# The first two tiles of a decoder step run side by side, chunk by chunk of x, behind four products of ones

## The chip, the core and the metric

One core of a Trainium2 chip runs the whole program in one launch. The metric is the device time of that launch in microseconds. The engines are named as the profile names them: PE is TensorE, PEld its weight load, DVE is VectorE, ACT is ScalarE, POOL is GpSimd, SP is SyncE (here it issues nearly all DMAs). `L491` is line 491 of the kernel before.

## What is computed

The reference is one step of a two-layer decoder trunk over 512 prompt tokens and 32 sample tokens, all in float32. The change touches only the start of the first SwiGLU block:

```python
def rmsnorm(x, g):
    y = x * lax.rsqrt(jnp.mean(x * x, axis=-1, keepdims=True) + EPS)
    return y * g

def swiglu(x, w1, w3, w2):
    return (jax.nn.silu(x @ w1) * (x @ w3)) @ w2

# layer i: half SwiGLU -> token mixer -> half SwiGLU -> gated embedding
h = h + 0.5 * swiglu(rmsnorm(h, ffn1_norm[i]), ffn1_w1[i], ffn1_w3[i], ffn1_w2[i])
```

## The kernel before

The residual stream `h` lies transposed: eight chunks of 128 features (partitions) by 544 tokens. Every product is made in three passes for float32 accuracy. Each operand is split in a high part (a cast to the multiply type, on ACT) and a low part (what is left over, on DVE), and PE multiplies high by high, high by low, low by high. `prep` (L297, L298) applies the norm's gain to a chunk of x and splits it. `_split` (L198, L199) splits one piece of weights: 128 by 1024 numbers, 512 KB. The rsqrt factor of the norm is applied later, to the result.

A **tile** is one output of 128 rows by 544 tokens in PSUM: eight chunks, three passes each, and every pass is a pair of matmuls over 256 and 288 columns (`mm`, L241, L245, L247), so 24 pairs. The first SwiGLU block starts with eight such plain tiles (`ffn`, with `plain` = 2, from the w1 and w3 columns in turn); after them comes a seven-product (Strassen) scheme at L491. Its products come in the order 1, 5, 6, 2, 7, 3, 4. Product 6 adds into the PSUM tile of product 1, so it has to wait until ACT has copied product 1 out (L499). Plain tiles have three PSUM buffers; ACT copies each finished tile out (L426), which frees its buffer.

The sums of squares for the norm (squares on ACT L1357, adds on DVE L1359) go through four matmuls with a matrix of ones (L362) and then through a chain on ACT (L340) and DVE (L343 to L347). That chain gives the factor `rstd`, and the gates (L451, L454, L457) and the operands of the seven-product scheme (L307, L311 to L314, L285, L286) stand behind or between it on the same two engines. In the kernel before, `tile_rstd` runs these four matmuls inside the first tile for which the loop of `ffn` asks; the scheduler puts them into the third tile.

What sets the order: each engine runs its own list in order. In the blocks under `manual_schedule` the list of the named engines is the order of the code; elsewhere the scheduler of the framework places instructions by its own estimate. DMAs of SP go out in SP's order, and at most eight of them can be open, since the ninth waits on the semaphore of the first. SP's list also holds register loads from a page table `pt` (L1030, a TENSOR_LOAD and two small instructions each), which wait until `pt` has landed and stand between the DMAs. Weights are loaded piece by piece in the order in which the tiles use them. I call them piece 0, 1, 2 and so on; tile 1 uses piece 0.

Of the kernel before, what the change touches and what calls it, by code (L numbers as in the profile page):

```python
# [22 lines left out]
F32 = mybir.dt.float32  # L23
F32R = mybir.dt.float32r
I32 = mybir.dt.int32
AF = mybir.ActivationFunctionType
ALU = mybir.AluOpType
AX = mybir.AxisListType

P = 128  # L30
D = 1024
NC_ = D // P
# [57 lines left out]
def whole(p):  # L90

    return p[:].rearrange("p a b -> p (a b)")[:, 512 - CUT:512 - CUT + T]


class Builder:
# [310 lines left out]
    def ffn(self, h, box, gcol, rstd, on_chunk, plain=1):  # L406

        nc, eng = self.nc, mybir.EngineType
        self.ahead = (2, 3, 6)
        first, xs, xf = [], self.pairs(box), box["f"]  # L410

        def more(n):
            if len(xf) < min(n, NKP):
                xf.append(self.forms(h, gcol, len(xf), xs))
        hid, todo = {}, ([], [])
        lead = plain == 1 and len(xf) < 3
        for f in range(2 * plain):
            g = self.big()
            for w in range(2):
                if lead:  # L420
                    more(len(xf) + 1)
                if rstd is None:
                    p, rstd = self.tile_rstd(xs, box["acc"])
                else:
                    p = self.tile_mm(xs)
                nc.scalar.copy(g[:, w], whole(p))  # L426
                for t in todo:
                    if t:
                        t.pop(0)()
                if not lead:  # L430
                    more((2 * f + w + 1) // plain)
            first.append((f // 2, f % 2, g))
            if f % 2 and f < 2 * plain - 1 or lead and f == 0:
                for j, a, g in first:
                    todo[a].extend(self.gate(hid, rstd, j, a, g))
                first = []
        assert self.chain is None
        for j, a, g in first:
            todo[a].extend(([None] * 3 if j == 0 else []) + self.gate(hid, rstd, j, a, g))
        with self.tc.manual_schedule(engines={eng.PE, eng.Activation, eng.DVE, eng.Pool}):  # L440
            self.ffn_steps(h, xf, rstd, hid, todo, plain, on_chunk)
        self.ahead = (2, 2, 4)
        self.pins = 2
        return rstd
# [853 lines left out]
    def build(self):  # L1298
        nc, i, o = self.nc, self.i, self.o
# [26 lines left out]
        nc.vector.memset(self.eps, EPS)  # L1326
        warm = self.sm(1)
        nc.scalar.copy(warm, self.eps)
        self._load()
        self.g = self.const.tile([P, NG], F32, name="gains")  # L1330
        nc.scalar.dma_start(out=self.g, in_=i["gains"])
        hp = [self.big() for _ in range(NC_ // 2)]
        h = [hp[c // 2][:, c % 2, :] for c in range(NC_)]
        for c in range(NC_):
            nc.sync.dma_start(out=h[c], in_=i["x"][c])
            if c == 2:
                self._load()
        self.ones = self.const.tile([P, 32], F32, name="ones")
        nc.gpsimd.memset(self.ones, 1.0)
        self.onesr = self.const.tile([P, P], F32R, name="onesr")  # L1340
# [8 lines left out]
        box = {"x": {}, "f": [], "acc": self.st()}  # L1349
        with self.tc.manual_schedule(engines={mybir.EngineType.Activation, mybir.EngineType.DVE}):  # L1350
            for c in range(NC_):
                box["x"][c] = self.prep(h[c], G_FFN1 + c)
                if c in (0, NC_ - 1):
                    self._split()
            for c in range(NC_):
                sq = box["acc"] if c == 0 else self.tmp()
                nc.scalar.activation(sq, h[c], AF.Square)  # L1357
                if c:
                    nc.vector.tensor_tensor(box["acc"], box["acc"], sq, ALU.add)  # L1359

        def constants():
            yield
            nc.sync.dma_start(out=self.c, in_=i["consts"])
            nc.sync.dma_start(out=self.pt, in_=i["pt"])
            passed = self.big()[:].rearrange("p a b -> p (a b)")
            nc.sync.dma_start(out=passed[:, :NPASS], in_=i["passed"])
            yield
            nc.gpsimd.tensor_copy(self.identr, self.ident)
            nc.gpsimd.tensor_copy(self.neg, passed[:, C_NEG:C_NEG + 384])
        self.bg.append(constants())  # L1370

        on, nxt = self.next_norm(h, G_MIX)
        self.ffn(h, box, G_FFN1, None, on, PLAIN[0])
        box = nxt
        on, nxt = self.next_norm(h, G_FFN2, early={1: 0, 3: 1, 5: 2})
        self.gmlp(h, box, on)
        box = nxt
        on, nxt = self.next_norm(h, G_PLE)
        self.ffn(h, box, G_FFN2, None, on)
        box = nxt  # L1380
# [3 lines left out]
        box = nxt  # L1384
        box, rstd = self.kv(h, box, G_FFN1 + 8)
        on, nxt = self.next_norm(h, G_MIX + 8)
        self.ffn(h, box, G_FFN1 + 8, rstd, on)
        box = nxt
        on, nxt = self.next_norm(h, G_FFN2 + 8, early={5: 0, 6: 1})
        self.attention(self.pairs(box), box["acc"], h, on)  # L1390
        box = nxt
        on, nxt = self.next_norm(h, G_PLE + 8)
        self.ffn(h, box, G_FFN2 + 8, None, on)
        box = nxt
# [120 lines left out]
```

## Time and profile before

| What | us |
|---|---|
| median of 3 runs (lowest, highest) | 2065.02 (2064.10, 2067.02) |
| the profiled execution | 2064.99 |
| its span, first to last instruction | 2063.2 |
| PE busy in the span | 2043.9 (99%) |
| DVE busy | 1507.6 (73%) |
| ACT busy | 949.2 (46%) |
| start of PE's first product | 6.94 |

The span leaves 1.8 us of the profiled execution outside. A row of a timeline says when a run of equal instructions started, how long it lasted from the first start to the last end, the engine, the line, and in brackets how long the engine had been idle and who ended that. Rows of matmuls overlap: a matmul's length includes the way through the array, and the distance between starts is the pace.

### The profile page before, as it was taken

The numbers are of one execution on the slowest core, as the hardware profiler recorded it, in microseconds if no ns is written. First come the engines' busy times: TensorE is split into PE (matmuls) and PEld (weight loads), VectorE is DVE, ScalarE is ACT, GpSimd is POOL, SyncE is SP. The second block draws the span as 40 slices with busy tenths as digits, with TensorE's granted clock in tenths as the row PEclk, the third lists the DMA queues.
The fourth block names the chain that finished last, engine by engine and source line by source line (L and its number), as shares of the span: only waits on it lengthen the run. The fifth ranks groups of instructions, "written<-read, shape, count | busy, mean of one in ns | idle before, by whom it ended". The sixth has DMA issues, their size and how long they took to land.

```text
span 2063.2 us, 38844 instructions
## 1 busy us (share of the span) xinstructions
PE 2043.9 (99%) x16432; PEld 2012.0 (98%) x16432; DVE 1507.6 (73%) x1869; ACT 949.2 (46%) x1405; POOL 186.9 (9%) x238
## 2 busy tenths in 40 slices
PE   8999999999999999999999999999999999999999
PEld 8999999999999999999999999999987999999999
DVE  7877777556687777776688777776476888777774
ACT  7534344423554344454456343434364754344451
POOL 0000000410100000043060000001142200000020
PEclk9999999999999999999999999999999999999999
DMA  5233234312223232432374322324669322322431
GB/s 185 84 110 108 73 108 141 97 44 83 83 92 113 73 106 80 153 99 82 109 260 156 112 93 102 108 71 130 201 208 305 103 101 82 104 103 82 128 99 44
DMA packets 93807, 237.95 MB, mean 115 GB/s; under 512 B 9522, under 2 KB 27474, under 8 KB 93634
## 3 DMA queue, kind: packets, MB, share of 16 engines
q1 hardware_dynamic: 93490, 235.44, 34.4%
q8 instruction: 129, 2.11, 0.4%
q14 instruction: 44, 0.36, 0.1%
q10 hardware_dynamic: 144, 0.04, 0.0%
HBM read 218.95 MB, written 16.49 MB: 114 GB/s over the span
## 4 chain that ended last, share of the span: by engine, by line
PE 93%; DVE 3%; ACT 2%; issue 1%; DMA 1%; SPq 0%; POOL 0%; DVEq 0%; ACTq 0%
PE ps L491 33%; PE ps L241 16%; PE ps L247 16%; PE ps L245 16%; PE pb L491 5%; DVE big L199 1%; PE ps L1265 1%; PE ps L1269 1%; PE ps L1268 1%; ACT big L198 1%; PE ps L1222 0%; DVE big L184 0%; PE ps L829 0%; PE ps L830 0%; PE ps L831 0%
## 5 line engine op out<-in xcount | busy, mean ns | idle before, releaser
L491 PE MATMUL ps<-big,big 128*128 128x272 f32 x5616 | 727.7, 288 | 1.8 <-DVE big L508 1.3
L491 PEld LDWEIGHTS ps<-big,big 128*128 128x128 f32 x5616 | 714.2, 188 | 2.4 <-issue 1.6
L199 DVE TENSOR_TENSOR big<-big,big 128x1024 fp32r<-128x1024 f32 (+2 forms) x538 | 592.2, 1103 | 106.6 <-ACT big L198 106.0
L198 ACT CAST big<-big 128x1024 fp32r<-128x1024 f32 (+2 forms) x538 | 488.0, 932 | 267.8 <-DVE big L184 262.8
L241 PE MATMUL ps<-big,big 128*128 128x256 f32 (+1 forms) x2684 | 559.0, 289 | 7.2 <-ACT big L198 7.2
L247 PE MATMUL ps<-big,big 128*128 128x256 f32 x2684 | 554.5, 288 | 1.3 <-DVE big L199 1.3
L245 PE MATMUL ps<-big,big 128*128 128x256 f32 x2684 | 554.0, 287 | 0.0
L241 PEld LDWEIGHTS ps<-big,big 128*128 128x128 f32 x2684 | 430.5, 189 | 10.7 <-ACT big L198 7.4
L245 PEld LDWEIGHTS ps<-big,big 128*128 128x128 f32 x2684 | 432.9, 189 | 0.0
L247 PEld LDWEIGHTS ps<-big,big 128*128 128x128 f32 x2684 | 429.8, 188 | 3.1 <-DVE big L199 2.7
L326 POOL TENSOR_TENSOR st<-st,tmp 128x544 f32<-128x544 f32 (+1 forms) x63 | 87.4, 1387 | 1589.1 <-ACT tmp L324 1589.0
L530 DVE SCALAR_TENSOR_TENSOR big<-ps,big 128x544 f32<-128x544 f32 x160 | 115.6, 723 | 106.5 <-PE ps L247 106.4
L184 DVE TENSOR_TENSOR big<-big,big 128x1024 f32<-128x1024 f32 x156 | 190.1, 1219 | 0.0
L499 ACT COPY tmp<-ps 128x544 f32<-128x544 f32 x117 | 71.7, 613 | 141.3 <-PE ps L491 141.3
L454 ACT ACTIVATE big<-big 128x544 f32<-128x544 f32 x88 | 58.0, 660 | 163.3 <-DVE big L451 162.1
L491 PE MATMUL pb<-big,big 128*128 128x272 f32 x936 | 124.0, 288 | 0.0
L451 DVE TENSOR_TENSOR big<-big,st 128x1088 f32<-128x1088 f32 x88 | 113.7, 1293 | 10.6 <-ACT big L513 8.9
L491 PEld LDWEIGHTS pb<-big,big 128*128 128x128 f32 x936 | 120.2, 188 | 0.0
L297 ACT ACTIVATE big<-big,gains 128x544 fp32r<-128x544 f32 (+1 forms) x80 | 55.8, 704 | 118.4 <-DVE big L530 64.9
L286 DVE TENSOR_TENSOR big<-big,big 128x544 fp32r<-128x544 f32 (+1 forms) x112 | 80.9, 728 | 36.2 <-ACT big L285 36.1
L298 DVE SCALAR_TENSOR_TENSOR big<-big,gains,big 128x544 fp32r<-128x544 f32 (+1 forms) x80 | 66.0, 832 | 26.1 <-ACT big L297 26.1
L285 ACT CAST big<-big 128x544 fp32r<-128x544 f32 (+1 forms) x112 | 71.3, 644 | 16.0 <-DVE big L457 8.9
(208 smaller groups left out, 1435.6 us busy)
## 6 DMA issues: line engine op xcount, KB each, us to landing
big<-in_w SPq DMA_DIRECT2D x156, 512.0 KB
big<-in_w2a SPq DMA_DIRECT2D x64, 512.0 KB
big<-in_w2b SPq DMA_DIRECT2D x32, 384.0 KB
big<-in_w13p SPq DMA_DIRECT2D x16, 512.0 KB
big<-in_win SPq DMA_DIRECT2D x16, 512.0 KB
big<-in_wg SPq DMA_DIRECT2D x16, 512.0 KB
big<-in_ck SPq DMA_DIRECT2D x16, 512.0 KB
big<-in_cv SPq DMA_DIRECT2D x16, 512.0 KB
```

Of the source, the lines that this page charges most:

```text
L184: self.nc.vector.tensor_tensor(t, a, b, ALU.add if op == "+" else ALU.subtract)
L198: self.nc.scalar.copy(hi, src)
L199: self.nc.vector.tensor_tensor(lo, src, hi.bitcast(F32), ALU.subtract)
L241: i = nc.tensor.matmul(out[:, a:b], wh, xh[:, a:b], start=s, stop=False)
L245: nc.tensor.matmul(out[:, a:b], wh, xl[:, a:b], start=False, stop=False)
L247: nc.tensor.matmul(out[:, a:b], wl, xh[:, a:b], start=False, stop=e)
L286: self.nc.vector.tensor_tensor(pair[:, 1, cols], src, pair[:, 0, cols].bitcast(F32), ALU.subtract)
L326: nc.gpsimd.tensor_tensor(acc[:, cols], acc[:, cols], sq, ALU.add)
L451: tt(g, g, rstd.unsqueeze(1).broadcast_to([P, 2, T]), ALU.mult)
L491: nc.tensor.matmul(dst[w], a[:, c], b, start=k in "152" and kp == 0 and n == 0, stop=kp == NKP - 1 and n == 2, skip_group_check=True)
L499: nc.scalar.copy(t["r" + k], t["C" if k == "5" else "A"])
L530: nc.vector.scalar_tensor_tensor(h[c], whole(out), 0.5, h[c], ALU.mult, ALU.add)
```

## The change

Three things change at the start of the program. First, PE gets four float32 products of a 128 by 256 tile of ones, whose result nobody reads, at the head of its list. Second, the first two weight pieces are no longer loaded whole around x. Each is loaded in two halves of 256 KB, and the halves are put between the chunks of x (behind chunks 0, 2, 3 and 5); ACT and DVE split a half as they come to it. Third, PE runs tiles 1 and 2 in turn: three chunks of tile 1, three of tile 2, then chunk 3 of both, chunk 4 of both, and so on. The loop of `ffn` takes these two tiles as done, so that its first call of `tile_rstd` comes with tile 3.

```diff
@@ ffn
             for w in range(2):
                 if lead:
                     more(len(xf) + 1)
-                if rstd is None:
+                if box.get("p"):
+                    self.prepare()
+                    p = box["p"].pop(0)
+                elif rstd is None:
                     p, rstd = self.tile_rstd(xs, box["acc"])
@@ build
-        self._load()
+        busy = self.flat(256)
+        nc.vector.memset(busy, 1.0)
+        t = self.pb()
+        for _ in range(4):
+            nc.tensor.matmul(t[:, :256], busy[:, :P], busy, start=True, stop=True)
+        w0 = [(self.flat(1024), self.flat(1024, F32R), self.flat(1024, F32R)) for _ in range(2)]
+        half = lambda k: slice(512 * k, 512 * k + 512)
         for c in range(NC_):
             nc.sync.dma_start(out=h[c], in_=i["x"][c])
-            if c == 2:
-                self._load()
+            for w, k in {0: [(0, 0)], 2: [(1, 0)], 3: [(0, 1)], 5: [(1, 1)]}.get(c, ()):
+                nc.sync.dma_start(out=w0[w][0][:, half(k)], in_=self.aps[w][:, half(k)])
+        self.a_load = self.p_split = self.p_sum = self.p_next = 2
@@ under manual_schedule of ACT and DVE
                 box["x"][c] = self.prep(h[c], G_FFN1 + c)
-                if c in (0, NC_ - 1):
-                    self._split()
+                for w, k in {0: [(0, 0)], 2: [(1, 0)], 3: [(0, 1)], 5: [(1, 1)]}.get(c, ()):
+                    raw, hi, lo = (t[:, half(k)] for t in w0[w])
+                    nc.scalar.copy(hi, raw)
+                    nc.vector.tensor_tensor(lo, raw, hi.bitcast(F32), ALU.subtract)
+            self._split()
@@ before the call of ffn
+        xs, b = self.pairs(box), [self.blocks(t[1:]) for t in w0]
+        box["p"] = [self.ps(), self.ps()]
+        with self.tc.manual_schedule(engines={mybir.EngineType.PE}):
+            for w, cs in ((0, range(3)), (1, range(3))) + tuple((w, [c]) for c in range(3, NC_) for w in range(2)):
+                self.mm(box["p"][w], [b[w][c] for c in cs], [xs[c] for c in cs], cs[0] == 0, cs[-1] == NC_ - 1)
```

How the lists of the engines move, at three places. The first is ACT behind the squares of x. Before, it casts piece 2 (`big_168`), copies tiles 1 and 2 out (`ps_182`, `ps_256`), makes the high part of the sum of squares (L357) and casts piece 3 (`big_174`):

```order
L1357 ACTIVATE tmp_163<-big_89 128x544
L198 CAST big_170<-big_168 128x1024 [waits DMAHW5_49]
L426 COPY big_167<-ps_182 128x544 [waits PE_49]
L426 COPY big_167<-ps_256 128x544 [waits PE_49]
L357 CAST tmp_225<-st_109 128x544 [waits DVE_49]
L198 CAST big_246<-big_174 128x1024 [waits DMAHW6_49]
```

After the change piece 2 is cast ahead of the squares; behind them stand the casts of piece 3 (`big_288`) and piece 4 (`big_294`), and only then the copies of tiles 1 and 2 (`ps_186`, `ps_187`):

```order
L1371 ACTIVATE tmp_182<-big_94 128x544
L198 CAST big_290<-big_288 128x1024 [waits DMAHW0_49]
L198 CAST big_296<-big_294 128x1024 [waits DMAHW1_49]
L429 COPY big_287<-ps_186 128x544 [waits PE_49]
L429 COPY big_287<-ps_187 128x544 [waits PE_49]
L307 ACTIVATE big_310<-big_91,gains 128x544 x2
```

So the copy of tile 1, which frees the PSUM buffer that tile 4 takes, now stands behind a cast that waits for the DMA of piece 4.

The second place is SP, from the constants and the page table `pt` on. Before, two register loads from `pt` stand ahead of the DMA of piece 2 (`big_168`):

```order
L1363 DMA consts<-in_consts 128x224 [waits DMAHW3_49]
L1364 DMA pt<-in_pt 1x16 [waits DMAHW4_49]
L1030 TENSOR_LOAD pt [waits DMAHW4_49]
L1030 ISA x2
L1030 TENSOR_LOAD pt
L1030 ISA x2
L165 DMA big_168<-in_w13p 128x1024 [waits DMAHW5_49]
```

After the change piece 2 (`big_157`) goes out ahead of the first register load:

```order
L1377 DMA consts<-in_consts 128x224 [waits DMAHW5_49]
L1378 DMA pt<-in_pt 1x16 [waits DMAHW6_49]
L165 DMA big_157<-in_w13p 128x1024 [waits DMAHW7_49]
L1033 TENSOR_LOAD pt [waits DMAHW6_49]
L1033 ISA x2
```

Piece 2 moved ahead of the loads. Behind it, five register loads now stand ahead of piece 3 and nine more ahead of piece 4, and six more ahead of piece 5; before, two stood ahead of piece 2, nine between pieces 2 and 3, and none between pieces 3, 4, 5 and 6.

The third place is PE where the four matmuls with ones for the norm (L362) stand. Before, they are inside tile 3 (`ps_331`), at its chunks 4 to 6:

```order
L247 MATMUL ps_331<-big_128,big_171 128x288
L362 MATMUL pb_229<-tmp_225,onesr 128x272 [waits Activation_49,Pool_49]
L362 MATMUL pb_230<-tmp_225,onesr 128x272
L241 MATMUL ps_331<-big_131,big_170 128x256
L241 MATMUL ps_331<-big_131,big_170 128x288
```

After, they are inside tile 5 (`ps_474`), at its first chunk and its second:

```order
L241 MATMUL ps_474<-big_125,big_296 128x256 [waits Activation_49]
L241 MATMUL ps_474<-big_125,big_296 128x288
L245 MATMUL ps_474<-big_125,big_296 128x256
L362 MATMUL pb_372<-tmp_368,onesr 128x272 [waits Activation_49,Pool_49]
L362 MATMUL pb_373<-tmp_368,onesr 128x272
```

They moved back by almost two tiles, and the chain for `rstd` with them. In the rows behind tile 8 the lists of PE, ACT and DVE are those of before, apart from a few neighbours that change places on DVE.

## Rows read from the trace of the kernel before

**Rows 1.** The page, its first line.

```profile
span 2063.2 us, 38844 instructions
```

**Rows 2.** PE's waits, whole span: who waited for whom, us, times, longest.

```profile
PE ps L241 <- ACT big L198: 7.2, 2, 6.9
PE pb L1241 <- DVE tmp L1237: 1.3, 1, 1.3
```

**Rows 3.** PE's timeline, tiles 1 and 2 and the start of tile 3.

```profile
6.94 0.82 PE L241 MATMUL ps<-big,big 128*128 128x256 f32 x2 [6.94 <-ACT big L198]
...
12.45 0.66 PE L247 MATMUL ps<-big,big 128*128 128x256 f32 x2
12.90 0.59 PE L241 MATMUL ps<-big,big 128*128 128x256 f32 x2
13.33 0.41 PE L245 MATMUL ps<-big,big 128*128 128x256 f32 x2
...
22.05 0.41 PE L241 MATMUL ps<-big,big 128*128 128x256 f32 x2
```

**Rows 4.** Busy time by stretch: PE, PEld, DVE, ACT, POOL, PEclk, DMA share, GB/s.

```profile
5.00:10.00 5.00, 3.06 (x12) 2.75 (x13) 3.40 (x4) 3.49 (x5) 0.00 (x0) 1.00 1.01 371
```

**Rows 5.** ACT's timeline: first chunk of x, and the chain for rstd.

```profile
5.21 0.75 ACT L297 ACTIVATE big<-big,gains 128x544 fp32r<-128x544 f32 x1 [2.57 <-DMA big<-in_x]
...
23.62 1.05 ACT L198 CAST big<-big 128x1024 fp32r<-128x1024 f32 x1 [0.22 <-DMA big<-in_w13p]
24.58 1.38 ACT L307 ACTIVATE big<-big,gains 128x544 f32<-128x544 f32 x2
25.98 1.28 ACT L340 ACT_TABLE_LOAD   x1
27.27 0.87 ACT L340 ACTIVATE st<-pb,eps 128x272 f32<-128x272 f32 x2
```

**Rows 6.** SP's timeline (issues of pt, pieces 2 and 3) and SP's wait.

```profile
7.46 0.30 SPq L1364 DMA_DIRECT2D pt<-in_pt  x1
13.22 0.36 SPq L165 DMA_DIRECT2D big<-in_w13p  x1
18.68 0.33 SPq L165 DMA_DIRECT2D big<-in_w13p  x1
...
SPq L1030 <- DMA pt<-in_pt: 4.0, 1, 4.0
```

**Rows 7.** DMA, 12 to 24 us, 40 slices of 0.3 us.

```profile
GB/s 9 0 0 0 0 0 0 82 0 150 287 273 410 382 164 0 0 0 0 0 0 0 0 0 0 109 109 177 218 314 369 396 382 410 410 437 423 423 437 423
```

**Rows 8.** PE's timeline: start of tile 4, start of the seven-product scheme.

```profile
28.52 0.41 PE L241 MATMUL ps<-big,big 128*128 128x256 f32 x2
...
58.74 6.96 PE L491 MATMUL ps<-big,big 128*128 128x272 f32 x54
```

**Rows 9.** DVE's timeline, from the rstd chain to the seven-product scheme.

```profile
28.17 0.72 DVE L343 SCALAR_TENSOR_TENSOR tmp<-st 128x544 f32<-128x544 f32 x1 [2.24 <-ACT st L340]
...
29.45 0.78 DVE L346 SCALAR_TENSOR_TENSOR tmp<-pb,tmp 128x272 f32<-128x272 f32 x2
30.15 0.43 DVE L313 TENSOR_TENSOR tmp<-big,tmp 128x272 f32<-128x272 f32 x1
...
32.12 1.29 DVE L451 TENSOR_TENSOR big<-big,st 128x1088 f32<-128x1088 f32 x1
33.32 0.72 DVE L286 TENSOR_TENSOR big<-tmp,big 128x544 fp32r<-128x544 f32 x1
...
62.95 2.36 DVE L199 TENSOR_TENSOR big<-big,big 128x1024 fp32r<-128x1024 f32 x2 [0.23 <-ACT big L198]
```

**Rows 10.** ACT's timeline up to the copy of the first of the seven products.

```profile
61.32 0.65 ACT L285 CAST big<-tmp 128x544 fp32r<-128x544 f32 x1 [1.22 <-DVE tmp L314]
61.87 2.00 ACT L198 CAST big<-big 128x1024 fp32r<-128x1024 f32 x2
63.77 0.61 ACT L499 COPY tmp<-ps 128x544 f32<-128x544 f32 x1
```

## The prediction

> **What bounds the kernel now.** I read the page's first line, then PE's waits, then the timelines of PE, ACT, SP and DVE up to the seven-product scheme. The span is 2063.2 us [rows 1] and PE works nearly all of it; its only long wait is the 6.9 us before its first product [rows 2]. So what the change can win lies in the first 22 us, and the question is whether PE can keep it.
>
> At the start PE is late and slow. Its first product starts at 6.94, the twelve pairs up to 12.90 take 5.96 us, 0.497 a pair, and undisturbed 0.45 (12.45 to 12.90). From 13.33 to 22.05 there are 35 pairs in 8.72 us, 0.249 each [rows 3]. 544 columns in 0.45 us is the lower level of TensorE's clock (1.2 GHz), and the second pace is the upper one, although the granted clock reads 1.00 in that stretch as well [rows 4]; before the rise PE had been working for 6 us, before that it had stood idle. The slow pairs cost 12 x (0.497 - 0.249) = 3.0 us. Tile 3 starts at 22.05.
>
> **Part 1: ones, halves, two tiles in turn.** The first chunk of x is ready for ACT at 5.21, behind 512 KB of weights [rows 5]. At 371 GB/s [rows 4] those are 1.4 us, so x comes at 3.8; behind it a half piece takes 0.7 us, its cast about 0.6, and the first real product starts near 5.3, 1.6 us earlier. The chunks and halves then come in about the time in which PE eats them: 48 pairs x 0.249 = 12.0 us. With some 0.9 us of early holds for low parts (an estimate) tile 2 ends at 18.2 if the clock is up from the first real product. If the ones do not raise it and twelve pairs are slow again, it ends at 5.3 + 12.0 + 3.0 = 20.3. So tile 2 ends 1.7 to 3.9 us earlier than before.
>
> The ones themselves do no harm. They stand ahead of everything on PE, while it has nothing else. Four float32 products have no row here. The cheapest reading is the pace of one of the present passes, 4 x 0.125 = 0.5 us; the dearest four passes each at the lower level, 4 x 4 x 0.21 = 3.4 us (256 columns of the 544 in 0.45 us). Either way they end by about 4.7, before 5.3. The extra casts and subtractions are the same numbers in halves: two more instructions on ACT and on DVE, some 0.1 us of overhead each, beside PE's work.
>
> **Part 2: where the gain meets a wait, tile 4.** Tile 3 needs piece 2, whose DMA now goes out ahead of the register loads, some 4 us earlier than 13.22 [rows 6]; it is there well before 18.2. Tile 3 ends 24 x 0.249 = 6.0 us after tile 2, at 24.2 to 26.3. Tile 4 takes the PSUM buffer of tile 1. ACT copies that out only behind the cast of piece 4, and piece 4's DMA now stands behind fourteen register loads. From rows: pt is issued at 7.46, takes 0.30 to issue, and SP waits 4.0 for it, so the loads start at 11.76; two loads end at 13.22 (1.46); the issue of piece 2 (0.36) and nine loads take 18.68 - 13.22 = 5.46, so a load is 0.567 [rows 6]. The same bytes are ahead of pt after the change, so I keep 11.76. Five loads: 11.76 + 1.46 + 3 x 0.567 = 14.92, the issue of piece 3. Issue and nine loads: 14.92 + 5.46 = 20.38, the issue of piece 4. For the landing there are two bounds: piece 2 went alone, issued at 13.22, and its bytes stopped at 16.5 (the fifteenth slice), 3.3 us [rows 6, 7]; piece 3 had three more right behind it and reached ACT at 23.62, 4.9 us after 18.68 [rows 5, 6]. Piece 4 goes alone, with six loads behind it, so I take 3.6: 24.0. Cast 0.95 (two in 1.90) and copy 0.61 [rows 10] give **25.6** for the start of tile 4, between 25.3 and 26.9. That is later than the 24.2 at which tile 3 would be done with a fast clock. Before, tile 4 started at 28.52 [rows 8] with the four matmuls L362 done (0.5 us); against 28.0, PE is 2.4 us ahead, whatever the clock did.
>
> **Part 3: where the rest meets a wait, the third of the seven products.** The rstd chain now hangs on tile 5 instead of tile 3, and on ACT it stands behind the copy of tile 4. Before, it reached DVE at 28.17, and the copy of the first product ended at 63.77 + 0.61 = 64.4 [rows 9, 10]. PE reached the third product (number 6), which needs that copy, at 58.74 + 48 x 0.126 = 64.8 (0.126 from 54 in 6.96) [rows 8]: a margin of 0.4 us. After, counted from tile 4's start: the tile 6.0; ACT's copy 0.61, L307 1.40, the table load 1.29, L340 0.90, together 4.2 [rows 5, 9, 10]. Then DVE has 32 instructions from L343 to the last L314: 14 of 544 columns at 0.64 (the two from 28.17 to 29.45), 8 of 272 at 0.35 (29.45 to 30.15), 4 of 1088 at 1.20 (32.12 to 33.32), 6 of 1024 at 1.14 (2.36 less the last one's 1.22) [rows 9]: 9.0 + 2.8 + 4.8 + 6.8 = 23.4. Where DVE must await a cast of ACT in between, the hand-overs cost 1.2 (a weight cast of 1.05 [rows 5] that nothing covers), 0.8 (a cast of 0.65 [rows 10]), 0.3 and two of 0.2 [rows 9]: 2.7. The last L314 needs 0.1 more than its distance to a successor; ACT then has 0.55 + 1.90 + 0.61 [rows 10]. Sum from L343: 23.4 + 2.7 + 0.1 + 3.1 = 29.3. From tile 4's start that is 6.0 + 4.2 + 29.3 = 39.5, so the third product starts at 25.6 + 39.5 = 65.1, against 64.8. PE alone would be there after five tiles of 5.98, the L362 at 0.5, some 0.4 of a hold at tile 7 and 6.0, 36.8 in all, at 62.4: it waits 2.7 us.
>
> From there on the lists are as before and ACT and DVE stand against PE as they stood, so nothing more is lost or won. **Sum:** 2064.99 + 0.3 = 2065.3, where the profiled execution (its span and 1.8 us around it) is as good as the median, 2065.02. With the bounds of the landing, 25.3 to 26.9, the sum goes from 2065.0 to 2066.6.
>
> **Rivals.**
> A, ACT and DVE are quicker than my count: the wait at the third product is gone, the one at tile 4 stays. PE gets to the third product at 62.4, a gain of 2.4: 2062.6. For it: the margin is a sum of 32 instructions, and 5% of it is 1.5 us. Against: their paces are measured, and DVE had idle time before mostly where PE made it wait.
> B, SP is quicker: pt lands earlier or piece 4 comes sooner, tile 4 starts at 24.2, and the third product at 24.2 + 39.5 = 63.7: 2063.9. Against it: the loads' pace is steady [rows 6].
> C, both: 24.2 + 36.8 = 61.0, 2061.2, close to the whole gain of the start.
> D, slower: the clock falls in the new waits of PE (1.4 us at tile 4, 2.7 at the third product). The rows give 3.0 us for one stretch at the lower level. One fall makes 2068.3, both 2071.3; it decides from the second. Against it: a wait of 1.3 us [rows 2] stands in a kernel whose granted clock is 1.00, though none as long as 2.7 is there. The Trainium skill (TensorE: Matmul & The Clock Gate, the table of "Why this matters for your kernels") warns of pauses between bursts after which the clock goes back to half. By that rule D's second wait would be near the danger; no row here shows it.
> E, the ones do not do what they are for: tile 2 ends at 20.3, tile 3 at 26.3, tile 4 starts there, the third product at 65.8: 2066.0. That lies in the range of my forecast. The Trainium skill (the same page, Part 1) says that the number of slow products at a start differs from run to run; by that, E can be true in one run and not in the next. The trace shows one start.
>
> **How the numbers follow.** The forecast with E 0.68 (2065.0 to 2066.6), A 0.12, B 0.11, C 0.05, D 0.04 (both falls 0.02). The likeliest time is 2065.3. A, B and the forecast hold 0.91; from 2062.4 to 2067.0. 0.2%, about 4.1 us, is what a measurement of this kernel can tell from no change: faster by more means under 2060.9, which only the good end of C reaches, 0.03; slower means over 2069.1, two falls, 0.03 with what I overlooked; within, 0.94.
>
> **What would show it.** Right: tile 2 ends near 18 to 20; PE idle before tile 4 until about 25.6, put down to ACT's copy, with ACT idle before a cast that waits for a weight DMA; L362 in tile 5; PE idle by 2 to 3 us in the seven-product scheme, put down to ACT's copy of its first product; tile 9 on as before, within 1 us. Wrong: PE without idle time after 25.6 (A), tile 4 at 24 or sooner (B), pairs of 0.45 us behind one of the waits (D).

## The result and the profile after

The changed kernel takes 2068.39 us (median of 22 runs, 2066.01 to 2071.61), the kernel before 2065.48 (22 runs beside it): a ratio of 1.0016, with a 95% interval of 1.0010 to 1.0022. So it is 2.9 us (0.16%) slower. Three executions in a far slower state, one of the variant with the late page table (2839.95 us) and two of the kernel before (2194.49 and 3339.46 us), are in no median and no count below. I had forecast 2065.3, within 2062.4 to 2067.0; the time lies above the range. The profiled execution took 2069.17.

| What | before | after |
|---|---|---|
| span of the profiled execution | 2063.2 | 2066.4 |
| outside the span | 1.8 | 2.8 |
| PE's first real product | 6.94 | 5.60 |
| start of tile 3 | 22.05 | 20.09 |
| start of tile 4 | 28.52 | 26.51 |
| start of the third of the seven products | 64.78 | 66.21 |

The first line of the page of after:

```profile
span 2066.4 us, 38868 instructions
```

And of PE's waits over the whole span of after (who waited for whom, us in total, times, longest) the two largest that are new, or longer than in [rows 2]:

```profile
PE ps L494 <- ACT tmp L502: 2.9, 2, 2.4
PE pb L1187 <- POOL big L1174: 1.8, 1, 1.8
```

The wait of 6.9 us ahead of the first product is gone, as meant. In its place PE waits 2.4 us at the third of the seven products for ACT's copy of the first (L494 and L502 are L491 and L499 of before). The 1.8 us for GpSimd stand in the sample attention, 1530 us later; I come back to them.

PE's timeline of after: the ones, the start of tile 1, the rise of the clock, the starts of tiles 3 and 4, the seven products (against [rows 3, 8]):

```profile
1.21 3.78 PE L1337 MATMUL pb<-big 128*128 128x256 f32 x8 [1.21 <-DVE big L1334]
5.60 0.82 PE L241 MATMUL ps<-big,big 128*128 128x256 f32 x2 [0.62 <-ACT big L1366]
...
9.75 0.66 PE L247 MATMUL ps<-big,big 128*128 128x256 f32 x2
10.21 0.59 PE L241 MATMUL ps<-big,big 128*128 128x256 f32 x2
10.63 0.41 PE L245 MATMUL ps<-big,big 128*128 128x256 f32 x2
...
20.09 0.41 PE L241 MATMUL ps<-big,big 128*128 128x256 f32 x2
...
26.51 0.52 PE L241 MATMUL ps<-big,big 128*128 128x256 f32 x2 [0.28 <-ACT big L429]
...
57.63 6.20 PE L494 MATMUL ps<-big,big 128*128 128x272 f32 x48
66.21 3.29 PE L494 MATMUL ps<-big,big 128*128 128x272 f32 x24 [2.38 <-ACT tmp L502]
```

Up to tile 4 PE is 2.0 us ahead of before, at the start of the seven products still 1.1, and at the third of them 1.4 us behind. The ones end at 5.0 (1.21 + 3.78), and the first real product starts 0.6 us after them, yet in this execution the pairs stay at 0.45 us until 10.2.

ACT's timeline of after (against [rows 5, 10]): the cast of piece 4, the copies of tiles 1 and 2 behind it, the rstd chain, the copy of the first of the seven products.

```profile
24.90 1.06 ACT L198 CAST big<-big 128x1024 fp32r<-128x1024 f32 x1 [3.41 <-DMA big<-in_w13q]
25.85 1.12 ACT L429 COPY big<-ps 128x544 f32<-128x544 f32 x2
...
36.00 0.87 ACT L340 ACTIVATE st<-pb,eps 128x272 f32<-128x272 f32 x2
...
65.56 0.60 ACT L502 COPY tmp<-ps 128x544 f32<-128x544 f32 x1
```

ACT stands idle for 3.4 us, waiting for the DMA of piece 4, and only then copies tile 1 out, which tile 4 needs. The chain is on ACT at 36.0, in the kernel before at 27.3.

SP's timeline of after (against [rows 6]): the issue of pt, of pieces 2 and 3 (two rows in one), of pieces 4 and 5.

```profile
8.24 0.31 SPq L1378 DMA_DIRECT2D pt<-in_pt  x1
8.87 7.44 SPq L165 DMA_DIRECT2D big<-in_w13p  x2
21.42 4.57 SPq L165 DMA_DIRECT2D big<-in_w13q  x2
```

SP's wait for pt, from the waits of after:

```profile
SPq L1033 <- DMA pt<-in_pt: 3.6, 1, 3.6
```

Piece 2 is issued at 8.87 and takes 0.36 to issue; with the wait of 3.6 the register loads start at about 12.8, not at 11.76 as before, and piece 4 goes out at 21.42, not at 20.38.

### The profile page after: what moved, and what is told of

Read it like the earlier page. It is cut to its first block, busy times and chain, and to the rows that moved or that the text cites. A ratio compares the mean times of both kernels' runs of the same rounds, so it can differ in the third digit from the quotient of the medians.

```text
span 2066.4 us, 38868 instructions
## 1 busy us (share of the span) xinstructions
PE 2047.7 (99%) x16440; PEld 2014.1 (97%) x16440; DVE 1508.0 (73%) x1872; ACT 951.4 (46%) x1407; POOL 186.1 (9%) x238
## 4 chain that ended last, share of the span: by engine, by line
PE 90%; DVE 3%; ACT 2%; DMA 2%; issue 1%; SPq 1%; POOL 0%; ACTq 0%; DVEq 0%
PE ps L494 32%; PE ps L241 15%; PE ps L247 15%; PE ps L245 15%; PE pb L494 5%; ACT big L198 1%; DVE big L199 1%; PE ps L1268 1%; PE ps L1272 1%; PE ps L1271 1%; PE ps L832 1%; PE ps L833 1%; PE ps L834 1%; DVE big L184 1%; PE ps L1225 0%
## 5 line engine op out<-in xcount | busy, mean ns | idle before, releaser
L494 PE MATMUL ps<-big,big 128*128 128x272 f32 x5616 | 728.0, 288 | 4.1 <-ACT tmp L502 2.9
L494 PEld LDWEIGHTS ps<-big,big 128*128 128x128 f32 x5616 | 714.3, 188 | 5.0 <-ACT tmp L502 3.3
L502 ACT COPY tmp<-ps 128x544 f32<-128x544 f32 x117 | 72.0, 615 | 141.0 <-PE ps L494 141.0
L494 PE MATMUL pb<-big,big 128*128 128x272 f32 x936 | 124.0, 288 | 0.0
L494 PEld LDWEIGHTS pb<-big,big 128*128 128x128 f32 x936 | 120.2, 188 | 0.0
```

What stands on the lines that cost most here:

```text
L494: nc.tensor.matmul(dst[w], a[:, c], b, start=k in "152" and kp == 0 and n == 0, stop=kp == NKP - 1 and n == 2, skip_group_check=True)
L502: nc.scalar.copy(t["r" + k], t["C" if k == "5" else "A"])
```

## The experiments

Two theories were open, and one doubt. **Chain**: the late rstd chain holds the third product, and that is the loss in every execution (1.4 us here). **Clock**: the granted clock falls behind PE's new waits. The profiled execution shows no fall (1.000), but the mean granted clock of the 22 executions is 0.999 or 0.998 in 18, and 0.001 of 2066 us is 2 us. The doubt was the 1.6 us that this trace loses in the sample attention: is it the change, or the draw of one profile?

### The same kernels once more

> The changed kernel once more, nothing left out. In its first trace PE starts the third of the seven products 1.4 us later than before (66.21 against 64.78), and gets another 1.6 us behind at one place in the sample attention (a wait for a copy of GpSimd behind a DMA of rows); the mean granted clock was 1.000, but most of its timed executions show 0.999 or 0.998. Theory CHAIN: the 1.4 us are in every execution (third product at 66.0 to 66.4), the 1.6 us are chance and need not come again. Theory CLOCK: in an execution with a clock under 1.000 the trace shows a stretch at the lower level of 2 to 6 us right behind the new wait of 2.4 us, and half of it is lost: 1 to 3 us. Theory SHIFT: the later start moves a transfer against PE, and the 1.6 us stand at the same place again. Median about 2068.4 by all three.

> The changed kernel once more, beside the one with the filled wait, on the same chip in turn with it: median 2067.9 to 2068.4, the clock at 0.999 or 0.998 in more than half of the executions. The third product starts 39.6 to 39.9 us behind tile 4, as in the four traces with the late chain so far (39.70, 39.80, 39.94, 39.59).

> The kernel before once more, for a second trace of it. All five traces of the changed kernel and its variants show PE waiting 0.6 to 1.8 us in the second sample attention for a copy of GpSimd that stands behind a DMA of rows (issue to landing 7.1 to 8.3 us for the second of three); the first trace of before has 0.17 us there (6.3 us). Theory SHIFT (the change brings it about): 0.2 us here again, rows DMA 6.3. Theory CHANCE (the first trace of before was a good draw): 0.5 to 1.5 us here, rows DMA over 7.

The changed kernel took 2067.91 and 2069.12 (ratios 1.0011 and 1.0016 to the runs of before beside them, intervals 1.0002 to 1.0020 and 1.0007 to 1.0025). In both traces PE reaches the third product late (66.70, 67.89), and in both the clock falls. In the second it is 41.25 us behind tile 4 (67.89 - 26.64), where I had 39.6 to 39.9: a fall behind the wait for tile 4 holds tile 4 itself up by 1.6 us, and 41.25 - 1.6 is 39.65. From the second, PE's timeline: the starts of tile 4 and of the third product, each with a wait ahead, and the fourth; then PE by stretch (PE, PEld, DVE, ACT, POOL busy, PEclk, DMA share, GB/s):

```profile
26.64 0.52 PE L241 MATMUL ps<-big,big 128*128 128x256 f32 x2 [2.02 <-ACT big L429]
...
27.77 0.66 PE L241 MATMUL ps<-big,big 128*128 128x256 f32 x2
28.22 0.66 PE L245 MATMUL ps<-big,big 128*128 128x256 f32 x2
...
67.89 4.81 PE L494 MATMUL ps<-big,big 128*128 128x272 f32 x24 [2.40 <-ACT tmp L502]
72.54 3.19 PE L494 MATMUL pb<-big,big 128*128 128x272 f32 x24
```

```profile
27.20:30.50 3.30, 3.30 (x17) 3.30 (x16) 2.15 (x5) 2.51 (x5) 0.00 (x0) 0.50 0.99 349
30.60:34.00 3.40, 3.40 (x29) 3.40 (x28) 2.63 (x4) 1.78 (x3) 0.00 (x0) 1.00 0.66 258
68.20:71.40 3.20, 3.20 (x16) 3.20 (x16) 2.49 (x4) 1.76 (x4) 0.00 (x0) 0.50 0.02 5
71.60:75.00 3.40, 3.40 (x29) 3.40 (x28) 3.19 (x5) 3.08 (x5) 0.00 (x0) 1.00 0.65 201
```

PEclk reads 0.50, the lower of the two levels, behind the wait of 2.02 us at tile 4, and again behind the wait of 2.40 us at the third product. Twenty-four products take 4.81 us there and 3.19 after it: one fall costs 1.6 us. In the other trace the clock stayed up behind 2.1 us at tile 4 and fell behind 2.5 us at the third product. Over all traces there are eight waits of 1.9 to 2.7 us at these two places. Behind four of them the clock falls (1.95, 2.02, 2.40 and 2.48 us), behind four it does not (2.10, twice 2.38, and 2.66 us, this last one without the ones). So a wait of this length is followed by a fall in some executions and not in others.

Over the executions whose clock was recorded, its mean is 1.000 in 124 of 127 of the kernel before and in 9 of 44 of the changed one. The time goes with it: of the 22 executions of the changed kernel in the section on the result, the four at 1.000 have a median of 2067.09 us, the thirteen at 0.999 one of 2068.37, the five at 0.998 one of 2069.53. So 1.6 us over the 2065.48 of before are lost without a fall, close to the 1.4 us by which the third product is late, and each 0.001 of clock goes with 1.2 to 1.3 us more.

The kernel before, traced a second time, waits 0.8 us in the sample attention where its first trace has 0.2. This is the row of the waits in the second trace:

```profile
PE pb L1184 <- POOL big L1171: 0.8, 1, 0.8
```

And in the first:

```profile
PE pb L1184 <- POOL big L1171: 0.2, 1, 0.2
```

In the other fifteen traces of this study it is between 0.3 and 1.8 us, whatever stands at the start of the program; in the kernel before with ones alone it is 0.6. The first trace of before was a good draw, and 1.8 is the longest of the seventeen, in a kernel whose two other traces have 0.9 and 1.1. So most of the 1.6 us is the draw of two profiles. Whether the change adds some tenths there, these traces can't tell.

### Without the ones, and the ones alone

```diff
-        for _ in range(4):
-            nc.tensor.matmul(t[:, :256], busy[:, :P], busy, start=True, stop=True)
```

> The changed kernel without the four products of ones; nothing else differs. If the ones do nothing for the clock (in the trace of the changed kernel the pairs come at 0.45 us up to 10.4): first product at 5.6, pairs at 0.45 up to 10.3 to 10.7, the rest as with the ones, and the median within 0.3 us of the changed kernel. If they do raise it early: before, the pace rose 6.3 us after the first product, so here at 5.6 + 6.3 = 11.9; 1.3 us more at the lower level are 0.65 us, of which the 0.3 us wait at tile 4 takes a part, so 0.3 to 0.6 us above the changed kernel.

> The kernel before plus the four products of ones at the head of PE; weights, tiles and chain as before. If the ones raise the clock early (4 to 6 us in three of four traces with them), the pairs of tile 1 come at 0.25 from about 7 on and tile 3 starts up to 3 us earlier, near 19. But the chain for rstd stands behind the cast of piece 3, whose DMA stands behind nine register loads: L343 at 28 as before, so the third product can come 0.4 us earlier at most: 64.4, median 2064.8 to 2065.3. A gain of over 1.5 us would say that PE is the bound up to there, against my sum.

Without the ones the kernel takes 2068.02 (1.0014, interval 1.0005 to 1.0023), as the changed one does (2067.91). Its pairs are at 0.45 us until 10.9, 5.7 us after the first product at 5.20. With the ones the first trace of after is little better (10.2), but it is the odd one out: in the thirteen other traces with ones the granted clock goes up between 4.2 and 6.7. So they mostly do what they are for, and the time does not show it, since PE only waits longer later: tile 4 starts at 26.89 without them and at 26.90 and 26.64 in the two later traces with them.

Ones ahead of the kernel before change nothing either, 2065.03 against 2065.09 (1.0000, interval 0.9991 to 1.0009). My bound there was too tight: in its trace the third product comes at 63.66, not at 64.4 or later, because ACT casts piece 3 at 22.33 (before 23.62 [rows 5]) and the chain is on ACT 1.1 us earlier. The trace also shows a fall at the start: the clock goes up during the ones (4.3), falls at 7.7 among the first products, which PE had awaited for 2.3 us, and pairs take 0.45 us from 8.9 to 10.7. Such falls make a mean of 0.999 too: 5 of the 11 executions show it, and they lose nothing (2065.00 against 2065.15 for the other six). So a mean of 0.999 alone does not say where the clock fell. But the variant without ones, whose clock rises only at 11.3 in its trace, is at 0.999 in 6 of 11, and in the changed kernel such executions are 1.3 us longer: there most of the falls probably stand behind the later waits.

### Register loads and the rstd chain, apart and together

The page table is loaded behind weight piece 6, so that SP's register loads stand behind the pieces:

```diff
-            nc.sync.dma_start(out=self.pt, in_=i["pt"])
+            with self.tc.issue_after(self.loads[6].ins):
+                nc.sync.dma_start(out=self.pt, in_=i["pt"])
```

The chain is asked for behind tile 1, and its four matmuls then stand in tile 3, as before the change:

```diff
                     p = box["p"].pop(0)
+                    if rstd is None:
+                        rstd = self.rstd(box["acc"])
```

> The changed kernel, but the page table is loaded behind the DMA of weight piece 6, so that no register load stands ahead of pieces 2 to 6. By my sum the wait at tile 4 is gone: it starts when tile 3 is done, at 26.1, and the third product 39.7 us later at 65.8, 0.4 earlier than in the changed kernel; PE still waits 2.4 to 2.7 us there. Median 0.4 us under the changed kernel, 2.5 above before. If SP's queue were the main cause instead, the third product would come at 64.8 or sooner and the median at 2065.5 or less. Theory CLOCK: the clock stays under 1.000 in most executions, since the wait stays. Where pt comes later, the first use of a page is hundreds of us away, which costs nothing.

> The changed kernel, but the chain for rstd is asked for behind tile 1, so that its four matmuls stand in tile 3, as before the change. Theory CHAIN: the chain leaves ACT at about 24.9 (cast of piece 4) + 0.95 + 2 x 0.61 + 1.4 + 1.3 + 0.9 = 30.6, needs 29.3 us from there (59.9), and PE comes to the third product at 26.5 + 36.8 = 63.3 without a wait, 1.5 us earlier than before. Median then 2065.5 - 1.4 = 2064.1, 4.3 us under the changed kernel if the clock or the shift belongs to the wait too, 2.9 under it if the other 1.4 us stay. Theory CLOCK: no wait over 1 us is left behind tile 4, so the mean clock is 1.000 in nearly all executions. Theory SHIFT: 1.6 us stay lost in the sample attention, median 2065.7. Against CHAIN: the third product stays at 66 with a wait of 2 us or more.

> The changed kernel with rstd asked for behind tile 1 and the page table loaded behind weight piece 6. In the variant with the early rstd alone the chain left ACT at 30.6, and between 24 and 30.6 DVE stood idle for 3.8 us behind the late piece 4; the third product came at 64.48 with a wait of 1.6 us. With piece 4 early: sum of squares done at 23.4, then on ACT 0.65 + 0.95 + 2 x 0.5 + 1.4 + 1.3 + 0.8 = 6.1, so the chain leaves ACT at 29.5 and the third product comes 1.1 us earlier, at 63.4. If DVE's and ACT's work on the operands behind it is the bound, PE still waits 1.5 to 2 us there, and the median is 1 us under the early rstd alone, 2064.3. If PE were the bound: 24.6 + 36.8 = 61.4 for the third product, median 2062.3.

| | tile 4 | third product | wait there | median | ratio, interval | executions at 1.000 |
|---|---|---|---|---|---|---|
| changed kernel (first trace) | 26.51 | 66.21 | 2.4 | 2068.39 | 1.0016 (1.0010 to 1.0022) | 4 of 22 |
| page table late | 24.93 | 64.52 | 2.4 | 2067.30 | 1.0010 (1.0000 to 1.0019) | 2 of 10 |
| rstd early | 26.68 | 64.48 | 1.6 | 2065.30 | 0.9999 (0.9990 to 1.0008) | 8 of 11 |
| both | 26.74 | 63.24 | 0.4 | 2064.40 | 0.9996 (0.9987 to 1.0005) | 9 of 11 |

The late page table shows the chain's rule most cleanly. The third product comes 64.52 - 24.93 = 39.6 us after tile 4; in the first trace of after it is 66.21 - 26.51 = 39.7, in the next 39.8, without ones 39.9. My sum had 39.5. It came earlier than I expected, since tile 3 was done at 24.9 in this execution (clock up from 5.9). And it shows the clock: the third product is 0.3 us earlier than in the kernel before, the profiled execution at 1.000 takes 2065.76, and still the median is 2.2 us above before (2067.3 against 2065.1), with the clock under 1.000 in 8 of 10.

With the early chain I was wrong by 1.2 us (64.48 for 63.3). It left ACT where I had it, 30.64 for 30.6:

```profile
30.64 0.73 DVE L343 SCALAR_TENSOR_TENSOR tmp<-st 128x544 f32<-128x544 f32 x1 [0.98 <-ACT st L340]
...
64.48 3.27 PE L496 MATMUL ps<-big,big 128*128 128x272 f32 x24 [1.62 <-ACT tmp L504]
```

(a row of DVE and one of PE, of that kernel). But 33.8 us stand behind it, not 29.3: splits and differences that DVE does ahead of the chain in the changed kernel now follow it (36 instructions of DVE from L343 to the last L314, where the changed kernel has 32). Moving the chain up reorders DVE's and ACT's work ahead of the third product, and only the part of their idle time that goes is won. Both edits together take a part of that idle time away too (63.24; I had 63.4). Its small wait there (0.4) flatters: PE was late itself, for a fall at the start.

### The sums of squares on GpSimd

```diff
-                    nc.vector.tensor_tensor(box["acc"], box["acc"], sq, ALU.add)
+                    nc.gpsimd.tensor_tensor(box["acc"], box["acc"], sq, ALU.add)
```

> As the variant with early rstd and late page table, but the seven sums of squares go to GpSimd (1.39 us each, from its other sums) instead of DVE (0.64 each): they end at 26, 2.5 us later than on DVE, and DVE has 4.5 us less to do. The chain then leaves ACT at 30.5, and behind it stands what stood behind it in the changed kernel: 29.3 us, so 59.8, earlier than PE at 61.4. If DVE's work is the bound of this stretch, the wait at the third product is gone, it starts at 61.4 to 62, 3 us earlier than before; median 2065.2 - 3 + 1 = 2063.2, with the 1 us of the sample attention still lost. If not, 64 or later again.

It took 2066.62 (1.0006, interval 0.9997 to 1.0015), 2.2 us more than without this edit, with the third product at 65.91. GpSimd's row:

```profile
17.24 11.81 POOL L1377 TENSOR_TENSOR st<-st,tmp 128x544 f32<-128x544 f32 x7 [2.82 <-ACT tmp L1375]
```

Seven sums take 11.8 us and end at 29.05, not at 26. The list of ACT changes as well: two casts of operands, a copy and a cast of weights now stand ahead of the chain, so it reaches DVE at 36.43, where I had 30.5 for its end on ACT. From there to the third product it is 29.5 us, and 29.3 in the changed kernel (66.21 - 36.90). So this run shows the 29.3 us of the sum once more; whether less work of DVE ahead of an early chain would help, it does not test.

### PE kept busy in the wait

Eighteen products of ones stand ahead of the third product (k is "6"), in a PSUM tile that is not yet in use:

```diff
+            if k == "6" and self.fill:
+                t["B"] = [self.pb()[:, :HT] for _ in range(2)]
+                for _ in range(self.fill):
+                    nc.tensor.matmul(t["B"][0], self.onesr, xf[0]["1"][0], start=True, stop=True, ...)
```

> The changed kernel, but in the wait at the third of the seven products PE does 18 products of a matrix of ones (128 by 272, 0.115 us each at the upper level, 2.1 us together), whose result nobody reads, into a PSUM tile that the next product but one overwrites; everything else waits for what it waited for before. Theory CLOCK (the fall of the clock behind the wait is the second half of the loss): the third product still starts at 66.2 to 66.8, but the clock does not fall behind it, nearly all executions show 1.000, and the median is 1.0 to 1.5 us under the changed kernel's in the same call. Theory CHAIN alone: PE's idle time there costs only itself, so filling it changes nothing: median within 0.3 us of the changed kernel's, clock as often under 1.000.

> The changed kernel with the page table loaded behind weight piece 6 and with the 18 products of ones in the wait at the third of the seven products. The chain for rstd stays in tile 5: third product at 24.9 + 39.6 = 64.5, 0.3 us earlier than before. If the late tile 4 and the fall of the clock are the whole loss, the median is that of the kernel before within 0.4 us (2064.9 to 2065.6), over 2 us under the late page table alone (2067.5), and nearly all executions show 1.000. If something else is in it, 2066.5 or more at a clock of 1.000.

Beside the changed kernel's 2069.12 the filled one takes 2067.03 (1.0009, interval 1.0000 to 1.0018), 2.1 us less (I had 1.0 to 1.5), and 8 of 11 executions are at 1.000 instead of 1 of 11. In its profiled execution the clock fell behind tile 4's wait, which is not filled, and not behind the third product. PE's timeline there:

```profile
65.59 2.39 PE L492 MATMUL pb<-big,onesr 128*128 128x272 f32 x18
68.16 3.28 PE L502 MATMUL ps<-big,big 128*128 128x272 f32 x24 [0.17 <-ACT tmp L510]
71.28 3.19 PE L502 MATMUL pb<-big,big 128*128 128x272 f32 x24
```

The same stretch by engine, for the clock (columns as above):

```profile
68.20:71.40 3.20, 3.20 (x25) 3.20 (x26) 2.49 (x3) 2.03 (x4) 0.00 (x0) 1.00 0.02 5
```

The 24 products take 3.28 us, where the control has 4.81. With the page table late as well, both waits of PE are gone and the chain stays where the change put it (tile 4 at 24.48, the third product at 64.08, 39.6 us later): 2065.49 (1.0001, interval 0.9992 to 1.0010), 1.8 us under the late page table alone, 9 of 11 executions at 1.000. This is the time of the kernel before. Nothing else is in the loss that these runs could tell.

### Can the gain be kept? Gates behind the operands

All gates of the plain tiles are put off behind the operands of the third product (on top of both edits above); then the same with five products of ones; then less is put off; then two weight pieces are split ahead of what is put off. Of the third and of the fourth variant these are the edits; that of the first is not shown:

```diff
@@ the loop of ffn keeps the last step of the first gates for later
-                    if t:
+                    if len(t) > (plain == 2):
                         t.pop(0)()
@@ ffn_steps, the same variant: two steps behind the first product
-                for f in t[:2 if (kind, at) == ("w", tail) and k > 0 else 1]:
+                for f in t[:2 if (kind, at) == ("w", tail) and k > 0 or plain == 2 and n == 0 else 1]:
@@ ffn_steps, the last variant only
+            if plain == 2 and n == 0:
+                self.prepare()
```

> The variant with early rstd and late page table, and the gates of the eight plain tiles put off as far as they can be: 5.4 us of DVE's work (four products of 0.64, two of 1.24, two splits of 0.64) now stand behind the operands of the third product instead of ahead of them. If DVE's and ACT's work from the chain on is the bound of that stretch, the operands are ready at 63.2 - 5.4 = 57.8 and PE is the bound: third product at 24.9 + 36.8 = 61.7 where the clock does not fall at the start, 63 where it does; 1.8 to 3.1 us earlier than before. If nothing that was put off is late in turn, the median is 2062.5 to 2063.5. Against it: the gates are needed by the first products of the second matrix, 9 us later, and could make PE wait there; then 2064.5 or more with a new wait near 85 us.

> As the variant with the gates put off, with five products of ones at the start instead of four. Four end at 4.7 and the first real product starts at 5.1 to 5.6; in two of seven traces the clock rose at 4.2 and fell again from 7.6 to 11.1 with the holds behind. A fifth ends at 5.2 to 5.6. If the gap ahead of the first real product makes the clock fall, the start is 1.2 to 1.7 us better in such executions and the median 0.3 to 0.8 us lower; if the holds inside tile 1 do it, nothing changes.

> The variant with early rstd and late page table, and of the gates only the split of the first pair (two casts, two subtractions of 0.64 us) and the next pair's product with rstd (two of 1.24 us) stand behind the operands of the third product, 3.8 us of DVE's work instead of 5.4. If DVE's and ACT's queue is what loses the gain, the third product comes at PE's own time, 61.7 to 62.5, 2.3 to 3.1 us earlier than before, without a wait over 1 us behind it, and the median is 2062.5 to 2063.5 against 2065.2 before. If the put-off work is late in turn, as with all gates put off: a wait over 1.5 us near 72, clock under 1.000, median over 2065.

> The variant with the first gates' split put off, and the weight pieces of the next two products split by DVE ahead of that work instead of behind it. In the trace of the former the third product started on time (61.16, 3.62 us earlier than before) and then held 0.9 us in its middle for the low part of its weights, which stood on DVE behind 3.8 us of gate work. If that queue is the cause, the hold is gone, PE stays 3 to 3.6 us ahead of the kernel before from the third product on, and the median is 2062.0 to 2063.3 (the former: 2064.07, its best execution 2062.3). If the gate work is late instead, a wait of 1 to 3 us comes at the second matrix near 67 to 72 and the median is 2064 or more.

| | third product | what waits next | median | ratio, interval | at 1.000 |
|---|---|---|---|---|---|
| all gates later | 61.68 | 3.6 us at 73.0 | 2069.97 | 1.0025 (1.0016 to 1.0034) | 0 of 11 |
| the same, five ones | 61.53 | 3.6 us at 72.8 | 2070.46 | 1.0025 (1.0016 to 1.0034) | 0 of 11 |
| first split and next product later | 61.16 | 0.9 us at 62.7 | 2064.07 | 0.9993 (0.9984 to 1.0002) | 9 of 11 |
| the same, weights first | 61.65 | 0.5, 0.4, 1.0 us at 69.9 to 76.3 | 2065.17 | 1.0000 (0.9991 to 1.0009) | 10 of 11 |

With all gates later the third product comes at PE's own time (61.68, where I had 61.7), without a wait: the queue of DVE and ACT was what held it. That the number agrees is in part luck: tile 4 came later (25.66 for 24.9) and PE took less from there (36.0 us for 36.8). Then the gates are late. PE's timeline at the second matrix, with all gates later:

```profile
68.97 0.41 PE L249 MATMUL ps<-big,big 128*128 128x256 f32 x2
73.00 0.82 PE L243 MATMUL ps<-big,big 128*128 128x256 f32 x2 [3.61 <-ACT big L287]
73.76 0.82 PE L247 MATMUL ps<-big,big 128*128 128x256 f32 x2
```

The stretch by engine in the same kernel:

```profile
71.60:78.20 6.60, 5.16 (x18) 4.33 (x19) 5.18 (x9) 2.40 (x4) 0.00 (x0) 0.50 0.42 146
```

A wait of 3.6 us is followed by a fall in every execution (the mean is 0.998 or less in 22 of 22 of these two variants), and PEclk reads 0.50 over 6.6 us. The fifth product of ones changed nothing that shows; its trace has no fall at the start, nor has that with four, so what makes the fall at the start stays open.

The best of all is the variant that puts off less: 2064.07, 1.2 us under before, with an interval that still holds no change; I had expected 2062.5 to 2063.5. PE holds for 0.9 us inside the third product, for a weight split that DVE does too late:

```profile
55.12 6.71 PE L498 MATMUL ps<-big,big 128*128 128x272 f32 x52
62.74 2.78 PE L498 MATMUL ps<-big,big 128*128 128x272 f32 x20 [0.91 <-DVE big L201]
```

Splitting that piece first removes the hold and brings three others, PE's rows at the second matrix and behind it:

```profile
69.85 0.52 PE L243 MATMUL ps<-big,big 128*128 128x256 f32 x2 [0.50 <-ACT big L287]
70.76 0.51 PE L247 MATMUL ps<-big,big 128*128 128x256 f32 x2 [0.39 <-DVE big L288]
...
76.25 0.49 PE L243 MATMUL ps<-big,big 128*128 128x256 f32 x2 [0.98 <-ACT big L200]
```

At 110 us PE is 2.4 us ahead of before in the better variant and 0.5 in the other. So there seems to be a limit behind the third product too: DVE and ACT have to finish this work before the second matrix, and these four orders only choose what waits. That no order keeps the gain is not shown. I expected 0.8 to 2.1 us from the last edit (2062.0 to 2063.3 against 2064.07); it lost 1.1.

## Why the prediction was wrong

**The start** held. The first real product starts at 5.60 (I had 5.3), the ones take 0.43 us a record, 3.4 us for their eight records, the dear end of my bounds, and end at 5.0 (I had 4.7), tile 2 ends at 20.09 (18.2 to 20.3). Rival E, that the ones do not raise the clock, is true in this trace and in no other with ones. The Trainium skill (TensorE: Matmul & The Clock Gate, Part 1) says that the number of slow products at a start differs from run to run; the three traces of the changed kernel agree, with the rise at 10.6, 6.2 and 6.7 us.

**Tile 4** was mis-sized: 25.6 forecast, 26.5 to 26.9 measured with SP's order unchanged. The term is the landing of pt. I kept 11.76, because the same bytes are ahead of it; the register loads start at about 12.8. Most of that is the issue of pt itself, 0.8 us later (8.24 for 7.46), behind two more DMAs on SP. Issue (21.42 for 20.38) and cast (24.90 for 24.0) follow at the distances I had. That is 0.9 us in the first trace, and the bounds of 25.3 to 26.9 held it.

**The third product** held: 39.7 us after tile 4 where the sum said 39.5, with a wait of 2.4 for 2.7. So the head loses 1.4 us in the first trace where I forecast 0.3; of the 1.1 us between them 0.9 come from tile 4.

**"From there on nothing is lost or won" failed.** This step cost the forecast: it put the clock behind the new waits at nothing. Rival D, the fall of the clock in these waits, had 0.04, and some fall shows in the mean clock of 35 of 44 executions. I had argued from a wait of 1.3 us in a kernel whose granted clock is 1.00 [rows 2]; that says nothing of 2.4 us, and I wrote so and still gave it next to no weight. The price was wrong the other way: 3.0 us a fall, taken from the slow pairs of the start, where one costs 1.6. By D's own place and the measured price the sum is 2065.0 + 1.4 + 1.6 = 2068.0, and from the 2065.48 of before beside it 2068.5; the median is 2068.39. Without a fall the four executions at 1.000 stand at 2067.09, above my range by 0.1 even so. The Trainium skill (the same page, "Why this matters for your kernels") names pauses between bursts after which the clock goes back to half; the traces agree that a pause does this, and show it for pauses shorter than those that the page warns of as well: behind four of eight waits of 1.9 to 2.7 us, and behind 3.6 us in both traces that have it. The two filled variants show that it is PE's idleness that matters there: same chain, no fall at the third product, 2 us less.

**One profile as the base.** Its wait of 0.2 us in the sample attention was a good draw, 0.8 in the second trace; the span of the profiled execution of after has 1.8 there. That made 1.6 us of its 3.2 us longer span. The median of before, too, was 2065.48 in the 22 executions beside the changed kernel, 0.5 above the 2064.99 from which my sum started.

**The rivals.** A, ACT and DVE quicker than counted, is refuted by the 39.6 to 39.9. B, SP quicker, is the variant with the late page table for tile 4 (24.93) and for the third product (64.52, where B had 63.7 from 24.2). C needs both; the variants that got near its 61.0 (61.16 to 61.68) wait later.

## What to carry to other kernels

A start that PE wins is worth nothing if the engines that feed it stand as late as before: count what must be done on them ahead of PE's next fixed point, and move their waits forward first. A new wait of PE can cost more than its length, since the products behind it may run at the lower level: here four of eight waits of 1.9 to 2.7 us brought 1.6 us more; look at the granted clock of every timed execution, not of the profiled one alone. Where such a wait can't be removed, products that nobody reads can stand in it: here they cost nothing, and the clock was at 1.000 in 17 of 22 executions.

## What was not expected of the hardware

Waits of equal length differ: behind 2.4 us at the third product the clock stayed up in the first trace of after and fell in the last, and without the ones it stayed up behind 2.7. A fall at the third product cost 1.6 us in both traces that have one (24 products in 4.81 instead of 3.19). GpSimd's seven sums of 128 by 544 took 11.8 us: five of them 1.36 us each, as its sums in the profile of before (1.39), and two 2.3 and 2.2. With ones on PE from 1.2 us on, the clock went up at 4.2 to 6.7 us in thirteen of fourteen traces, and in two of these it fell again at 7.6 to 7.7, among first products with holds of 0.2 to 2.3 us.
